# Delta-rule q, k and v turned by 32x32 blocks on DVE and over DRAM, decay chain with operands in PSUM, and a new slab order

## The chip, the core and the metric

The kernel runs on one core of one Trainium2 chip. Its engines are TensorE (PE; its weight loads are shown as PEld), VectorE (DVE), ScalarE (ACT), GpSimd (POOL) and SyncE (SP), which issues nearly all DMAs here. Each engine works through its own instructions in a fixed order and waits on semaphores for the others. SBUF is the on-chip working memory of 128 partitions; PSUM holds the results of matmuls. The metric is the device time of one execution in microseconds, as the median of several runs.

## What is computed

One layer of a hybrid encoder on 512 tokens of width 1024, in float32. The branch that the change touches is the gated delta rule: 8 heads of width 128, run forward and backward in chunks of 64 tokens.

```python
h = rms_norm(x, norm_pre)
(aq, ak, av, az, dq, dk, dv, db, da, dz, gate_att, gate_dn) = split_cols(h @ w_in)
...
qkv = silu(short_conv(concatenate([dq, dk, dv], -1), conv_w))      # 5 taps along the tokens
cq, ck, cv = qkv[..., :DN_KW], qkv[..., DN_KW:2 * DN_KW], qkv[..., 2 * DN_KW:]
qd = l2_norm(heads(cq)) * (DN_DK ** -0.5)
kd = l2_norm(heads(ck))
vd = heads(cv)
g = -exp(a_log) * softplus(da + dt_bias)                           # decay, per token, direction and head
beta = sigmoid(db)
o_dn = bidir_gated_deltanet(qd, kd, vd, g, beta)
o_dn = rms_norm(o_dn, dn_norm)
y_dn = (o_dn * silu(dz)) @ w_br_dn
...
mix = (sigmoid(gate_att) * y_att + sigmoid(gate_dn) * y_dn) @ w_out
x = x + rms_norm(mix, norm_post)
x = x + rms_norm(sigmoid(x @ w_ple_gate) * (p @ w_ple_proj), ple_norm)
```

Attention (8 query heads, 2 key heads, rotary) is the other branch; the change leaves it alone.

## The kernel before

**Products.** A float32 product of large matrices is made of three TensorE products of rounded parts: a weight slab of 1024 x 128 is loaded raw (wraw), ACT rounds it (whi), DVE or POOL subtract (wlo), and gemm_t (lines 529 to 531) sums lo x hi, hi x lo and hi x hi over 8 steps of 128 rows: 24 matmuls of 512 columns for one slab. gemm_n (548 to 550) and gemm_k (566 to 568) do the same for weights that stream. Small products (the delta rule's) are plain float32 matmuls, which appear as two TensorE instructions each; a transpose is one.

**The delta rule's way.** For each of 24 slabs dq0..7, dk0..7, dv0..7, conv_job runs gemm_t and spawns conv_tail. There, conv_silu2 scales the middle tap on ACT, adds four taps on DVE (scalar_tensor_tensor from PSUM), takes tanh on ACT and one more product on DVE. The result has features on partitions and tokens along a row. conv_tail then needs tokens on partitions: transposed (line 758) makes four 128x128 transposes on TensorE into a PSUM bank. For dk and dq, ACT squares them, DVE sums over the features (ssk, ssq), and for dk ACT copies the tile out (kn). For dv, DVE multiplies by the key norm into nv. k_stats and q_stats turn the sums into norms on POOL. Two groups of four heads follow each other: prep makes the decay factors E, phase_a the products kk and qk (938, 943), the masks, and the inverse of a triangular matrix by a chain of small DVE steps and by block products (1015 to 1063), and phase_b the walk over four chunks in two directions (kS 1097, oq 1108, pw 1117, pS 1135, oa 1149). In phase_b, kn is the stationary operand of line 1135; nv streams at line 1117 in the first step and is read by DVE at 1101 in the others.

**decay** (its small products at 665, 697 and 724) makes g and beta for all heads early on: 17 DVE operations of at most 64 elements a partition, on tiles gv and beta in SBUF, with an exponential and a logarithm on ACT between them. TensorE's line 697 waits for its end.

**What sets the order.** Nothing is scheduled at run time. While the program is built, the class Flow plays all these generators against each other with a planned duration for each operation, and each engine's instructions come out in the order of planned times. ORDER lists the slabs as TensorE's gemm stream takes them; PR holds priorities; caps holds the number of buffers (5 PSUM banks mm, 3 banks aux, 5 SBUF tiles f2). Two weight buffers and some spare ones (SPARE) let loads run ahead. W marks DVE operations that are planned so that POOL is idle beside them. warm_up (1773) makes TensorE transpose an identity until WARM, before the first product arrives.

## Time and profile before

| what | value |
|---|---|
| median of 3 runs | 764.97 us (763.32 to 765.44) |
| the profiled execution | 764.65 us, of which its span (first to last instruction) 762.9 us |
| granted TensorE clock, mean | 0.998 |
| bytes moved by DMA | 102.59 MB, 54472 packets |
| share of the 16 DMA engines, SP's queue | 41.0% |

The profile's page gives the busy time of each engine and its share of the span, the same in 40 slices, the chain of work that ended last (followed back from the last instruction, at each step to what released it), the groups of instructions by line with busy time, mean duration, the idle time ahead of them and what ended it, and the DMA issues with the time to landing. Views of the trace give waits (who waited for whom, in total, how often, the longest), timelines, and busy time in chosen windows. In a row, L758 is line 758 of the kernel; `mm<-ident,u` is an output tile and what it was made of. Operations recorded by the planner's helpers all carry a helper's line (L122, L97, L102), so they are told apart by tile.

### The profile page before, as it was taken

Reading aid. Unit: us, or ns where it says so; the run is one execution under the profiler, and the core shown is the slowest. Engines: PE = TensorE matmul, PEld = TensorE weight load, DVE = VectorE, ACT = ScalarE, POOL = GpSimd, SP = SyncE. Lnnn points to the kernel's source line nnn. Section 1 sums busy time; section 2 is a strip of 40 time slices with the busy share of each in tenths; the row PEclk is TensorE's granted clock in tenths of the full one; section 3 lists DMA queues with packets and bytes.
Section 4 is the critical chain, followed back from the end, with each engine's and each line's share of the span. In section 5 each row is a group of like instructions: output and inputs, shape, how many; then the busy total and the mean of one; then the engine's idle time right before and its main releaser. Section 6 shows DMA issues by size and latency. Waiting matters only on the chain.

```text
span 762.9 us, 11833 instructions
## 1 busy us (share of the span) xinstructions
PE 747.1 (98%) x4501; PEld 625.0 (82%) x4501; DVE 470.3 (62%) x907; ACT 346.4 (45%) x649; POOL 307.4 (40%) x277
## 2 busy tenths in 40 slices
PE   8999999999999999999999999999999999999996
PEld 7678888878789888888788888888888888888885
DVE  4788688886965567895874535437666743413334
ACT  6668635443644255423442245335566632332422
POOL 4735753103223255202711245557355434661511
PEclk9999999999999999999999999999999999999999
DMA  8851527636121136545311134435324255653313
GB/s 344 284 170 43 172 81 245 183 127 223 40 71 42 44 123 180 193 143 148 112 57 40 44 111 139 139 110 194 110 82 167 85 184 193 198 152 128 97 60 120
DMA packets 54472, 102.59 MB, mean 134 GB/s; under 512 B 21072, under 2 KB 22032, under 8 KB 54416
## 3 DMA queue, kind: packets, MB, share of 16 engines
q1 hardware_dynamic: 54128, 101.58, 41.0%
q8 instruction: 35, 0.57, 0.3%
q10 hardware_dynamic: 288, 0.26, 0.1%
q14 instruction: 21, 0.17, 0.1%
HBM read 82.92 MB, written 18.91 MB: 133 GB/s over the span
## 4 chain that ended last, share of the span: by engine, by line
PE 87%; DVE 4%; DMA 3%; ACT 3%; issue 1%; POOL 1%; SPq 0%; POOLq 0%; DVEq 0%; ACTq 0%
PE mm L529 16%; PE mm L531 15%; PE mm L530 15%; PE mm L550 4%; PE mm L548 4%; PE mm L549 4%; PE mm L567 2%; PE mm L568 2%; PE mm L566 2%; PE aux L1117 2%; PE mm L1472 2%; PE aux L1149 2%; PE aux L1097 1%; PE aux L1108 1%; PE aux L1135 1%
## 5 line engine op out<-in xcount | busy, mean ns | idle before, releaser
L102 POOL TENSOR_TENSOR wlo<-wraw,whi 128x1024 fp32r<-128x1024 f32 x52 | 124.5, 2395 | 256.9 <-ACT whi L122 221.8
L529 PE MATMUL mm<-u,wlo 128*128 128x512 f32 x504 | 204.7, 406 | 1.8 <-DVE f L122 1.1
L531 PE MATMUL mm<-u,whi 128*128 128x512 f32 x504 | 197.2, 391 | 0.0
L530 PE MATMUL mm<-u,whi 128*128 128x512 f32 x504 | 196.5, 390 | 0.0
L529 PEld LDWEIGHTS mm<-u,wlo 128*128 128x128 f32 x504 | 94.8, 188 | 20.6 <-issue 1.9
L531 PEld LDWEIGHTS mm<-u,whi 128*128 128x128 f32 x504 | 94.6, 188 | 20.8
L530 PEld LDWEIGHTS mm<-u,whi 128*128 128x128 f32 x504 | 95.0, 188 | 17.0
L122 ACT CAST whi<-wraw 128x1024 fp32r<-128x1024 f32 x64 | 67.1, 1049 | 85.8 <-PE mm L531 55.3
L122 DVE SCALAR_TENSOR_TENSOR f<-mm,cw,f 128x510 f32<-128x510 f32 (+1 forms) x96 | 71.8, 748 | 16.9 <-ACT f L122 14.2
L102 POOL TENSOR_TENSOR u<-wraw,u 128x1024 fp32r<-128x1024 f32 x23 | 55.0, 2398 | 22.2 <-ACT u L122 22.1
L122 DVE TENSOR_TENSOR u<-aux,u 128x512 f32<-128x512 f32 (+2 forms) x60 | 39.3, 670 | 24.8 <-ACT u L122 15.2
L548 PE MATMUL mm<-u,u 128*128 128x512 f32 (+1 forms) x136 | 52.0, 382 | 0.0
L550 PE MATMUL mm<-u,u 128*128 128x512 f32 (+1 forms) x136 | 51.4, 378 | 0.0
L549 PE MATMUL mm<-u,u 128*128 128x512 f32 (+1 forms) x136 | 51.3, 377 | 0.0
L122 ACT COPY c<-aux 128x512 f32<-128x512 f32 x18 | 10.6, 589 | 55.0 <-DVE f L122 35.0
L122 ACT CAST u<-aux 128x512 fp32r<-128x512 f32 (+1 forms) x28 | 15.6, 556 | 39.8 <-PE aux L1645 12.9
L566 PE MATMUL mm<-whi,u 128*128 128x512 f32 x80 | 31.6, 395 | 0.0
L567 PE MATMUL mm<-wlo,u 128*128 128x512 f32 x80 | 31.3, 391 | 0.0
L568 PE MATMUL mm<-whi,u 128*128 128x512 f32 x80 | 31.2, 390 | 0.0
L122 ACT ACTIVATE mm<-f 128x512 f32<-128x512 f32 x24 | 14.4, 599 | 35.5 <-DVE f L122 34.1
L122 ACT CAST u<-wraw 128x1024 fp32r<-128x1024 f32 x24 | 25.1, 1050 | 11.6 <-DMA wraw<-in_wn_dram 10.1
L550 PEld LDWEIGHTS mm<-u,u 128*128 128x128 f32 x136 | 25.6, 188 | 4.8
(258 smaller groups left out, 1456.1 us busy)
## 6 DMA issues: line engine op xcount, KB each, us to landing
wraw<-in_wt_dram SPq DMA_DIRECT2D x60, 512.0 KB, 3.6
wraw<-in_wn_dram SPq DMA_DIRECT2D x28, 512.0 KB, 3.9
u<-in_wt_dram SPq DMA_DIRECT2D x12, 512.0 KB, 5.5
u<-CI SPq DMA_DIRECT2D x16, 256.0 KB, 6.2
u<-in_x_dram SPq DMA_DIRECT2D x4, 512.0 KB, 7.0
u<-in_xT_dram SPq DMA_DIRECT2D x4, 512.0 KB, 8.2
eD<-u SPq DMA_DIRECT2D x8, 256.0 KB, 8.1
gate_dz<-go SPq DMA_DIRECT2D x8, 256.0 KB, 2.1
```

The costliest lines, as they stand in the source:

```text
L102: ins = fn(*a, **k)
L122: fn(*a, **k)
L529: pe.matmul(o, lo[:, k, :], mh(k), start=(k == 0), stop=False)
L530: pe.matmul(o, hi[:, k, :], ml(k), start=False, stop=False)
L531: pe.matmul(o, hi[:, k, :], mh(k), start=False, stop=(k == 7))
L548: pe.matmul(o, b, hi, start=(i == 0), stop=False)
L549: pe.matmul(o, a, lo, start=False, stop=False)
L550: pe.matmul(o, a, hi, start=False, stop=(i == 7))
L566: pe.matmul(o[t], b, hi, start=(k == 0), stop=False)
L567: pe.matmul(o[t], a, lo, start=False, stop=False)
L568: pe.matmul(o[t], a, hi, start=False, stop=(k == 7))
L1117: pe.matmul(pw[:, h, :], Vm[g][d][:, 4 * c + h, :], r[:, h, :], start=True, stop=True)
```

## The change

**Turning the tiles.** transposed goes out of conv_tail. In its place one DVE instruction transposes the 128 x 512 result in 32x32 blocks (small_blocks), into a tile T in which the four chunks j of a token row lie side by side. For dq, T is squared and summed over the 32 features of each block: four partial sums for each token on the four blocks of partitions. The function sums adds them by four small matmuls with `four`, four stacked 32x32 identities. For dk the same is done, and T is also written to DRAM in one DMA and read back in four (turned), which puts the blocks together: kn[g][:, h] now has the shape token x feature x chunk, so the feature step is four elements. For dv, T goes over DRAM into nv[g][:, h] in the same shape, and the product with the key norm is made there, by POOL or by ACT, whichever the planner finds free. phase_b reads the new shapes.

**decay.** The tiles z, e, u, dd and the unfinished beta move to a PSUM bank of mm; mk, a reciprocal, a product and max(z, 0) stay in SBUF (gs). The absolute value and the sign change of exp(a_log) go from DVE to ACT.

**Order.** A new ORDER, new priorities and a longer WARM (5.5 instead of 4.6: 20 transposes instead of 16); a few events wait for the later of two times.

```diff
 ORDER = """
-dq3 dk2 dq2 dk0 dk3 dq0 dk1 dq1 dz2 dk7 dq6 dz3 dv2 dv1 dv3 dz0
+dk3 dk1 vec dq2 dq0 dq1 dq3 dk2 dz4 dk0 dv3 dv1 dq4 dv2 dq5 az6
...
-PR = dict(dec=6, dm1=5, y=2, conv=9, gate=1, kv=2, q=4, head=9, ple=6, prep=6, tab=2)
+PR = dict(dec=3, dm1=3, y=2, conv=4, gate=5, kv=7, q=8, head=6, ple=6, prep=7, tab=9)
...
-WARM = 4.6
+WARM = 5.5
...
-    two = const([64, 32], "two")
-    pool.tensor_add(two, ident[0:64, 0:32], ident[0:64, 32:64])
+    four = const([128, 32], "four")
+    pool.tensor_add(four, ident[:, 0:32], ident[:, 32:64])
+    for i in (2, 3):
+        pool.tensor_add(four, four, ident[:, 32 * i:32 * i + 32])
+    two = four[0:64, :]
...
-    gv = const([128, 5, 2, 4, 8], "gv")
+    gs = const([128, 4, 2, 4, 8], "gs")
...
-        z, e, u, dd, mk = (gv[:, i] for i in range(5))
+        yield "get", "mm"
+        gv = bank("mm", [128, 5, 2, 4, 8])
+        z, e, u, dd, bt = (gv[:, i] for i in range(5))
+        mk, dr, es, zr = (gs[:, i] for i in range(4))
...
-        t = V(0.15, t, dve.scalar_tensor_tensor, out=e, in0=z, scalar=-1.0, in1=z, op0=ALU.mult, op1=ALU.max)
+        t = A(0.25, t, act.activation, e, z, AF.Abs)
...
+    def small_blocks(src, dep):
+        T = tile("f2", [128, 4, 32, 4])
+        return T, V(0.64, dep, dve.transpose, T.rearrange("p a q j -> p j a q"), src)
+
+    def turned(T, dep, name, dst):
+        B = dram(name, [4, 32, 4, 128])
+        tw = Q(2, dep, B.rearrange("P i a n -> (P i) a n"), T.rearrange("p a q j -> p a (q j)"))
+        t = tw
+        for a in range(4):
+            t = Q(WIDE, tw, dst[32 * a:32 * a + 32].rearrange("p (P q) j -> p P (q j)", P=4), B[:, :, a, :].rearrange("P i n -> i P n"))
+        return tw, t
...
-        yield "at", t + 0.3
-        pt = yield from transposed(dst)
+        yield "at", t - 0.5
+        yield "get", "f2"
+        T, t = small_blocks(dst, t)
         if kind == "dv":
-            free("f2")
+            free("f2", t)
+            tw, t = turned(T, t, f"B{kind}{hd}", nv[g][:, h])
+            free("f2", tw)
             yield "ev", nke
-            t = V(0.62, 0.0, dve.tensor_mul, nv[g][:, :, h, :], pt,
-                  nk[:, g, :, h].unsqueeze(2).to_broadcast([128, 4, 128]))
...
+            def scaled():
+                for j in range(4):
+                    act.activation(n_[:, :, j], n_[:, :, j], AF.Copy, scale=nk[:, g, j, h:h + 1])
+
+            return either(t, ("POOL", 1.1, pool.tensor_mul, n_, n_, by), ("ACT", 1.25, scaled))
         if kind == "dk":
-            ta = A(0.5, ta, act.copy, kn[g][:, :, h, :], pt)
+            tw, t2 = turned(T, t, f"B{kind}{hd}", kn[g][:, h])
...
+        ta = A(0.5, t, act.activation, sq, T, AF.Square)
+        t = V(0.62, ta, dve.reduce_sum, parts_[kind][:, g, :, h, :], sq.rearrange("p a q j -> p a j q"), axis=AX.X)
...
+    def sums(kind, g):
+        yield "at", F.now + 0.3
+        yield "get", "mm"
+        o = bank("mm", [128, 16])
+        for a in range(4):
+            pe.matmul(o[32 * a:32 * a + 32, :], four, parts_[kind][:, g, a].rearrange("p h j -> p (h j)"), start=True, stop=True)
+        yield "pe", 0.44
+        return o.rearrange("p (h j) -> p j h", h=4)
...
-                kn[g] = unit((6, 9)[g], [128, 4, 4, 128])
+                kn[g] = unit((6, 9)[g], [128, 4, 128, 4])
...
-                nv[g] = unit(u, [128, 4, 4, 128])
+                nv[g] = unit(u, [128, 4, 128, 4])
...
-                    in1=nv[g][:, c, h, :], op0=ALU.mult, op1=ALU.add))
+                    in1=nv[g][:, h, :, c], op0=ALU.mult, op1=ALU.add))
...
-                r = nv[g][:, c]
+                r = nv[g][:, :, :, c]
...
-                    pe.matmul(pS[:, h, :], kn[g][:, c, h, :], wd[:, h, :], start=True, stop=True)
+                    pe.matmul(pS[:, h, :], kn[g][:, h, :, c], wd[:, h, :], start=True, stop=True)
```

Three places in the engines' orders. First DVE in the decay chain, right behind TensorE's line 665 (f is the conv tile of the first slab, gv and h are the chain's tiles). Before:

```order
L122 TENSOR_TENSOR gv<-mm_378,h_88 128x64
L122 SCALAR_TENSOR_TENSOR gv<-gv 128x64
L122 SCALAR_TENSOR_TENSOR f_46_374<-mm_297,cw,f_46_374 128x510
L122 SCALAR_TENSOR_TENSOR f_46_374<-mm_297,cw,f_46_374 128x511 x2
L122 SCALAR_TENSOR_TENSOR f_46_374<-mm_297,cw,f_46_374 128x510
L122 TENSOR_SCALAR gv<-gv 128x64
L122 TENSOR_SCALAR beta<-beta 128x64
L122 TENSOR_SCALAR gv<-gv 128x64 x2
L122 SCALAR_TENSOR_TENSOR u_38_291<-mm_297,f_46_374 128x512
L122 TENSOR_TENSOR gv<-gv 128x64
L122 RECIPROCAL gv<-gv 128x64
L122 TENSOR_TENSOR gv<-gv 128x64 x3
```

Now, at the same place (mm_387 is the chain's PSUM bank):

```order
L122 TENSOR_TENSOR mm_387<-mm_382,h_90 128x64
L122 TENSOR_SCALAR gs<-mm_387 128x64
L122 SCALAR_TENSOR_TENSOR f_47_380<-mm_303,cw,f_47_380 128x510
L122 SCALAR_TENSOR_TENSOR f_47_380<-mm_303,cw,f_47_380 128x511 x2
L122 SCALAR_TENSOR_TENSOR f_47_380<-mm_303,cw,f_47_380 128x510
L122 TENSOR_SCALAR mm_387<-mm_387 128x64 x3
L122 TENSOR_SCALAR gs<-mm_387 128x64
L122 SCALAR_TENSOR_TENSOR u_38_296<-mm_303,f_47_380 128x512
L122 TENSOR_TENSOR mm_387<-mm_387,gs 128x64
L122 RECIPROCAL gs<-mm_387 128x64
L122 TENSOR_TENSOR gs<-mm_387,gs 128x64
L122 TENSOR_TENSOR mm_387<-mm_387,gs 128x64 x3
```

The sequence is nearly the same; each small operation now reads the PSUM bank. Second, DVE some 20 us later, among the conv tails of the first slabs (f are conv tiles and turned tiles, u_38, u_47 and u_56 the units of kT and qT, u_68 and u_69 those of E). Before:

```order
L122 TENSOR_REDUCE ssk<-f_73_550 128x4
L122 SCALAR_TENSOR_TENSOR u_38_291<-mm_430,f_64_498 128x512
L122 SCALAR_TENSOR_TENSOR f_74_566<-mm_499,cw,f_74_566 128x510
L122 SCALAR_TENSOR_TENSOR f_74_566<-mm_499,cw,f_74_566 128x511 x2
L122 SCALAR_TENSOR_TENSOR f_74_566<-mm_499,cw,f_74_566 128x510
L889 TENSOR_TENSOR u_69_512<-u_69_512,cj 128x512
L122 SCALAR_TENSOR_TENSOR u_47_375<-mm_499,f_74_566 128x512
L122 TENSOR_REDUCE ssq<-f_77_605 128x4
```

Now:

```order
L122 SCALAR_TENSOR_TENSOR u_56_437<-mm_438,f_63_498 128x512
L122 STREAM_TRANSPOSE f_72_542<-u_38_296 128x4x128
L122 SCALAR_TENSOR_TENSOR f_74_563<-mm_499,cw,f_74_563 128x510
L122 SCALAR_TENSOR_TENSOR f_74_563<-mm_499,cw,f_74_563 128x511 x2
L122 SCALAR_TENSOR_TENSOR f_74_563<-mm_499,cw,f_74_563 128x510
L122 STREAM_TRANSPOSE f_76_585<-u_56_437 128x4x128
L122 SCALAR_TENSOR_TENSOR u_56_437<-mm_499,f_74_563 128x512
L122 TENSOR_REDUCE sm<-f_76_585 128x4x4
L122 TENSOR_REDUCE partk<-f_77_591 128x4x4
L947 TENSOR_TENSOR u_69_512<-u_69_512,cj 128x512
```

Each conv tail has one 512-element operation more, the block transpose, and its reduction gives 4 x 4 sums instead of 4. Third, SP's queue at the start of the decay factors' loads (wraw and u_29 are weight slabs, u_68 and u_69 the tiles of E). Before:

```order
L122 DMA wraw_495<-in_wt_dram 128x1024
L122 DMA CI<-f_67_510 64x128
L122 DMA wraw_542<-in_wt_dram 128x1024
L122 DMA u_68_511<-CI 128x512
L122 DMA u_69_512<-CI 128x512
```

Now:

```order
L122 DMA wraw_507<-in_wt_dram 128x1024
L122 DMA Bdk_458<-f_58_457 128x512
L122 DMA CI<-f_67_510 64x128
L122 DMA wraw_547<-in_wt_dram 128x1024
L122 DMA u_39_297<-Bdk_458 32x4x128 x4
L122 DMA u_68_511<-CI 128x512
L122 DMA u_69_512<-CI 128x512
L122 DMA Bdk_543<-f_72_542 128x512
```

The write of a turned tile and the four reads back stand among the weight loads and the loads of E; the reads come one or two rows behind the write. Line numbers after the change: gemm_t is 533 to 535, sums 847, pw 1182, pS 1200.

More of the change, by code (lines that the diff above doesn't have):

```diff
@@ L173 @@
 EOUT = 24.0
+WIDE = 2.0
 LONG, NEAR = 0.6, 1.5
 X_DVE = ()
-WARM = 4.6
+WARM = 5.5
 W1 = 0
@@ L682, in decay @@
         t = V(0.15, t, dve.tensor_add, dd, dd, mk)
[L683 to L684 removed]
+        t = V(0.5, t, dve.reciprocal, dr, dd)
+        t = V(0.15, t, dve.tensor_mul, es, e, dr)
         t = V(0.15, max(t, tl), dve.tensor_add, u, u, mk)
[L686 to L692 removed]
+        t = V(0.15, t, dve.tensor_mul, u, u, es)
+        tz = V(0.15, th, dve.tensor_scalar, out=zr, in0=z, scalar1=0.0, scalar2=None, op0=ALU.max)
+        t = V(0.15, max(t, tz), dve.tensor_add, u, u, zr)
+        ta = A(0.2, ta, act.mul, h16[:, 0:16], h16[:, 0:16], -1.0)
+        tg = V(0.15, max(t, ta), dve.tensor_mul, gg, u, ha)
+        t = V(0.15, tb, dve.tensor_scalar, out=bt, in0=bt, scalar1=1.0, scalar2=None, op0=ALU.add)
+        t = V(0.5, t, dve.reciprocal, beta, bt)
+        free("mm", max(t, tg))
         yield "at", tg + 0.3
@@ L800, in k_stats @@
             yield "ev", e
+        o = yield from sums("dk", g)
+        t = V(0.2, 0.0, dve.tensor_scalar, out=nk[:, g], in0=o, scalar1=4.0 * EPS, scalar2=None, op0=ALU.add)
+        free("mm", t)
         yield "ev", dec
-        t = G(0.2, 0.0, pool.tensor_scalar, out=nk[:, g], in0=ssk[:, g], scalar1=4.0 * EPS, scalar2=None, op0=ALU.add)
         t = V(0.25, t, dve.reciprocal, kinv[:, g], nk[:, g])
@@ L816, in q_stats @@
             yield "ev", e
-        return rsqrt(16, 0.0, rq[:, g], 1.0, 4.0 * EPS, float(128 ** -0.5), ssq[:, g])
+        o = yield from sums("dq", g)
+        t = V(0.2, 0.0, dve.tensor_copy, rq[:, g], o)
+        free("mm", t)
+        return rsqrt(16, t, rq[:, g], 1.0, 4.0 * EPS, float(128 ** -0.5))
     conv_ev, stat_ev = {}, {}
@@ L900, in prep @@
         if away:
+            t = max(tE[g, d, c] for c in range(NT))
             free("u16", t)
@@ L947, in phase_a @@
                 t = V(0.62, tE[g, d, c], dve.tensor_mul, AT[g][d][:, 4 * c:4 * c + 4, :], qk, E)
-                t = V(0.62, t, dve.tensor_mul, E, kk, E)
-            free("aux", t)
-            free("aux", t)
+                tm = max(tm, V(0.62, t, dve.tensor_mul, E, kk, E))
+            ready = max(ready, tm)
+            free("aux", tm)
+            free("aux", tm)
+        t = ready
         dB, dW = dram(f"dB{g}", [128, 32, 32]), dram(f"dW{g}", [128, 32, 32])
```

63 lines of the change are left out of this document (34 added, 29 removed).

## The prediction

> **What bounds the kernel now.** I read the busy shares first, then the slices, then the chain that ended last.
>
> ```profile
> span 762.9 us, 11833 instructions
> PE 747.1 (98%) x4501; PEld 625.0 (82%) x4501; DVE 470.3 (62%) x907; ACT 346.4 (45%) x649; POOL 307.4 (40%) x277
> PE   8999999999999999999999999999999999999996
> PE 87%; DVE 4%; DMA 3%; ACT 3%; issue 1%; POOL 1%; SPq 0%; POOLq 0%; DVEq 0%; ACTq 0%
> ```
>
> TensorE is busy in every slice and is 87% of the chain. A busy engine that overlaps its own instructions could still hide a slack, so I looked at how it steps: in the chain in order of time a 512-column matmul holds 0.23 us, and by the view of waits little interrupts them:
>
> ```profile
> 201.37 0.23 PE mm L530
> ```
>
> ```profile
> PE aux L697 <- DVE gg L122: 1.4, 1, 1.4
> ...
> PE mm L758 <- DVE f L122: 1.1, 1, 1.1
> PE mm L529 <- DVE f L122: 1.1, 1, 1.1
> PE aux L1097 <- ACT c L122: 0.5, 1, 0.5
> ...
> PE aux L1028 <- issue: 0.2, 1, 0.2
> ```
>
> Beside the first 6.27 us and the tail behind the last matmul (code that does not change), the list of ten holds 1.4 + 1.1 + 1.1 + 0.5 + 0.4 + 0.4 + 0.3 + 0.2 = 5.4 us of waiting. So the kernel is a TensorE queue, and a TensorE instruction taken out of it shortens the run by its own slot, as long as nobody becomes late.
>
> **The change part by part.** Base: the profiled execution, 764.65 us (span 762.9 plus 1.75 around it); the median shown is 764.97, 0.3 above it.
>
> *Transposes off TensorE.* `transposed` goes: 24 conv tails with four transposes each.
>
> ```profile
> 50.77 0.44 PE mm L758 x4
> L758 PE MATMUL mm<-ident,u 128*128 128x128 f32 x64 | 9.7, 273 | 0.1
> ```
>
> Two thirds of them, 64, are in the second row; its busy sum (9.7) counts the 0.27 us latency of each group, while the chain shows the slot, 0.44 for four. 24 x 0.44 = **-10.6**. The 1.1 us wait goes with its instruction.
>
> *Sums over four partition blocks.* Four groups of four small matmuls (32 TensorE instructions, as a float32 matmul is two) are new. The nearest rows bound them:
>
> ```profile
> 44.01 1.08 PE aux L697 x8
> 202.53 0.65 PE aux L1028 x48
> 214.80 2.01 PE aux L1048 x64
> ```
>
> With 128 stationary columns, (1.08 - 0.28) / 7 = 0.114 us each, or 3.6 in all; 32x32 tiles step by (0.65 - 0.19) / 47 = 0.01, 0.3 in all. 64x64 tiles at (2.01 - 0.22) / 63 = 0.028 lie nearest to 32 stationary columns: **+0.9**, bounds 0.3 and 3.6.
>
> *Start.* The first stream of matmuls is slow:
>
> ```profile
> 1.41 3.68 PE L1773 MATMUL mm<-ident 128*128 128x128 f32 x16 [1.41 <-POOL ident masks.py:199]
> 6.27 0.76 PE L1238 MATMUL mm<-u,u 128*128 128x512 f32 x1 [1.18 <-DVE u L97]
> ...
> 9.39 0.44 PE L1239 MATMUL mm<-u,u 128*128 128x512 f32 x1
> ```
>
> ```profile
> 19.39 1.24 DVE wlo L97
> ```
>
> From 6.27 to 9.39 seven steps take 3.12 us instead of 7 x 0.23 = 1.6. Twenty warm-up transposes instead of 16 end at 1.41 + 20 x 0.23 = 6.0, so the gap of 1.18 nearly closes and the first real matmul still starts at 6.27. At best 1.5 us is won; but the chain at 17 to 22 us lies on DVE, ACT and POOL (the 19.39 row), so most of an early finish would be waited away there. I take **-0.5**, bounds 0 and -1.5. [...]
>
> *Decay chain in PSUM.* DVE's small operations stand still behind POOL here:
>
> ```profile
> 31.70 2.35 DVE L122 SCALAR_TENSOR_TENSOR gv<-gv 128x64 f32<-128x64 f32 x1
> 33.99 3.11 DVE L122 SCALAR_TENSOR_TENSOR f<-mm,cw,f 128x510 f32<-128x510 f32 x4
> 37.02 1.72 DVE L122 TENSOR_SCALAR gv<-gv 128x64 f32<-128x64 f32 x1
> ...
> 40.55 2.71 DVE L122 TENSOR_TENSOR gv<-gv 128x64 f32<-128x64 f32 x3
> ```
>
> ```profile
> 31.56 2.41 POOL L102 TENSOR_TENSOR wlo<-wraw,whi 128x1024 fp32r<-128x1024 f32 x1 [1.04 <-ACT whi L122]
> 33.93 4.75 POOL L102 TENSOR_TENSOR u<-u,u 128x1024 fp32r<-128x1024 f32 x2
> 40.38 2.40 POOL L102 TENSOR_TENSOR wlo<-wraw,whi 128x1024 fp32r<-128x1024 f32 x1 [1.70 <-ACT whi L122]
> ```
>
> Operations of 64 elements take 2.35 and 1.72 us and end when POOL's two-input subtractions end (34.05 at 33.97, 38.74 at 38.68), and the three at 40.55 are held up likewise until 42.78; the conv steps at 33.99, with one operand in PSUM, run through POOL's 4.75 us at their usual 0.75 each. With z, e, u, dd and beta in PSUM every small operation of this chain has an operand there. That frees about 2.1 + 1.5 + 2.1 = 5.7 us of DVE (each stall less the 0.2 of a free one). The way from L665 to L697, 12.5 us now, becomes some 7, and TensorE still has 45 matmuls there (10.3 us, 0.44 less than now), so the 1.4 us wait goes: with L758's, **-2.5**.
>
> *DVE and the queue.* DVE gains 24 block transposes and loses eight products.
>
> ```profile
> L122 DVE SCALAR_TENSOR_TENSOR f<-mm,cw,f 128x511 f32<-128x511 f32 x48 | 36.0, 750 | 1.7
> L122 DVE STREAM_TRANSPOSE c<-u 32x512 f32<-32x512 f32 x8 | 5.6, 703 | 0.1
> L122 DVE TENSOR_REDUCE ssk<-f 128x4 f32<-128x512 f32 x8 | 5.4, 683 | 0.8 <-ACT f L122 0.7
> L122 DVE TENSOR_TENSOR u<-mm,nk 128x512 f32<-128x512 f32 x8 | 5.5, 682 | 0.3 <-PE mm L758 0.3
> 30.30:122.00 91.70, 90.20 (x463) 75.47 (x463) 73.89 (x112) 54.92 (x116) 54.65 (x46) 1.00 0.43 135
> ```
>
> 24 x 0.70 - 8 x 0.68 = +11.4 us of DVE, hidden beside TensorE if DVE keeps up. The tightest stretch runs from the decay chain to the last E product of group 0. There the new order has 13 conv tails (13 x (4 x 0.75 + 0.69) = 48), 13 block transposes (9.1), 10 reductions (6.8), 21 other 512-element operations (14.4) and about 3 us of small ones: **81 us of DVE against about 91 us of TensorE** (354 matmuls at 0.23, eight times 0.89 for the kk and qk groups, 3 us else). Today about the same stretch is the window quoted last: 73.89 of 91.70 us busy. DVE keeps up, with 10 us to spare. Uncovered, each microsecond beyond those 10 is one of the total. The 80 new DMAs go through SP's queue; what they bring is needed only by phase_b, which in the new order has more than 60 us of TensorE work ahead of it behind the last dv slab of either group, so their landing costs nothing. What remains of today's waits (5.4 - 2.5 = 2.9) I keep, and since every place in the order is new I add **+3.0** for new waits, bounds -2.9 (all gone) and +8.
>
> Sum: -10.6 + 0.9 - 0.5 - 2.5 + 3.0 = -9.7, so 764.65 - 9.7 = **755.0 us**. With every term at its good end: -10.6 + 0.3 - 1.5 - 2.5 - 2.9 = -17; but all of these together is unlikely, and I end the forecast's own range at 750, and at 759 above.
>
> **The rivals.** The new tiles kn and nv keep the four chunks of a token row side by side, so that TensorE reads kn[:, h, :, c] and nv[:, h, :, c], and DVE the squares and nv, one element in every 16 bytes. No TensorE row of before reads so. DVE has one pair: the solve's first step has 30 elements in 30 rows, 128 bytes apart, its last 30 side by side; and 58 elements in pairs:
>
> ```profile
> L973 DVE TENSOR_TENSOR blk<-blk,blk 128x30 f32<-128x30 f32 x1 | 0.2, 216 | 0.0
> L973 DVE TENSOR_TENSOR blk<-blk,blk 128x30 f32<-128x30 f32 x1 | 0.2, 191 | 0.0
> L973 DVE TENSOR_TENSOR blk<-blk,blk 128x58 f32<-128x58 f32 x1 | 0.2, 221 | 0.0
> L973 DVE TENSOR_TENSOR blk<-blk,blk 128x58 f32<-128x58 f32 x1 | 0.2, 220 | 0.0
> ```
>
> Apart costs (216 - 191) / 30 = 0.83 ns per element more; pairs (221 to 220) cost nothing. Thirty elements are few, and a row's end could be what costs.
>
> *Rival 1, slower: strided reads on TensorE.* L1135 loads kn as its weights.
>
> ```profile
> L1135 PE MATMUL aux<-f,u 128*128 128x128 f32 x96 | 13.0, 279 | 0.2
> 226.96 0.89 PE aux L1135 x8
> ```
>
> If each of its 96 loads of 128 columns, and the 32 first-chunk passes that stream nv, took 128 x 0.83 = 0.107 us more, that is 128 x 0.107 = 13.6 us: 755.0 + 13.6 = **768.6**. It decides from about 0.7 of that price (9.7 / 128 = 0.076 us a load), where it eats the whole gain. Against it: those slots (0.89 / 8 = 0.11) may have room to hide a slower read. Chance 0.20. [...]
>
> *Rival 2: DVE becomes the bound.* The same price on DVE alone: 23 transposes and reductions in the tight stretch x 512 x 0.83 ns = 9.8 us, all of its spare 10, and 48 steps of phase_b that read nv at +0.1 = 5. Half of this waited for, 7 us: **762**. The five PSUM banks are held longer, and TensorE waits at L529 and in kk and qk. Chance 0.20.
>
> *Rival 3: SP's queue.* Each of 16 heads writes to DRAM and, a row or two later, reads back, and the read waits in the queue until the write has landed; weight loads stand behind it.
>
> ```profile
> gate_dz<-go SPq DMA_DIRECT2D x8, 256.0 KB, 2.1
> L122 ACT CAST whi<-wraw 128x1024 fp32r<-128x1024 f32 x64 | 67.1, 1049 | 85.8 <-PE mm L531 55.3 <-PE mm L568 11.8 <-issue 8.4
> ```
>
> A landing is 2.1 us and the weight split waits for TensorE's buffers, not for loads, so 2 us of delay fits. If a quarter of it came through: 16 x 0.5 = 8, **763**. Chance 0.10.
>
> **How the numbers follow.** Forecast 755.0 (750 to 759) 0.50; rival 1 (766 to 772) 0.20; rival 2 (757 to 765) 0.20; rival 3 (757 to 767) 0.10. A measurement tells 0.3% from no change: below 762.7 is faster, above 767.3 slower. Faster: 0.50 + 0.13 + 0.05 = 0.68. Within: 0.03 of rival 1, 0.07 of rival 2, 0.05 of rival 3 = 0.15. Slower: 0.17. The range 750 to 767.5 leaves out the upper part of rival 1 (0.16) and about 0.03 below.
>
> **What would show it.** TensorE's busy time near 737 and waits under 6 us: forecast. L1200's groups of eight at 0.89 us: rival 1 is wrong; near 1.7: right. Block transposes at 0.70 and reductions at 0.68: rival 2 is wrong; near 1.1, with waits of L533 for DVE: right. ACT casts waiting for wraw: rival 3. The small operations on mm at 0.2 us each confirm the decay step, and the starts between 6.27 and 9.4 the warm-up. I am wrong if TensorE's slot does not shrink with the transposes, or if new waits exceed 8 us.

## The result, and the profile after

| | before | after |
|---|---|---|
| median | 765.21 us (763.32 to 765.72, 4 runs) | 784.32 us (782.69 to 785.27, 4 runs) |
| ratio | | 1.0252, 95% interval 1.0227 to 1.0277 |
| span of the profiled execution | 762.9 us | 782.9 us |
| TensorE busy / span less busy | 747.1 / 15.8 us | 757.3 / 25.6 us |

The change makes the kernel 2.5% slower; forecast were 755.0 us, and 767.5 as the upper end. The page of the changed kernel, its busy shares and its chain:

```profile
span 782.9 us, 11886 instructions
PE 757.3 (97%) x4441; PEld 633.8 (81%) x4441; DVE 490.8 (63%) x923; ACT 350.7 (45%) x649; POOL 321.0 (41%) x284
PEclk9999999999999999998999999999999999999998
PE 81%; DVE 7%; DMA 4%; ACT 3%; issue 2%; POOL 2%; SPq 1%; POOLq 0%; DVEq 0%; ACTq 0%
```

TensorE has 60 instructions fewer (96 transposes less, 32 for the sums and 4 of the warm-up more) and is busy 10.2 us *longer*; beside that it stands idle 9.8 us longer. Both parts have to be explained. The first is read from the groups of instructions by line and shape (busy time in us, mean of one in ns, then the idle time ahead):

```profile
L1200 PE MATMUL aux<-f,u 128*128 128x128 f32 x96 | 24.1, 394 | 0.1
L1182 PE MATMUL aux<-u,u 128*128 128x128 f32 x32 | 7.7, 404 | 0.0
L122 DVE STREAM_TRANSPOSE f<-u 128x512 f32<-128x512 f32 x16 | 17.7, 1103 | 0.1
L122 DVE TENSOR_REDUCE partk<-f 128x16 f32<-128x512 f32 x8 | 8.5, 1063 | 1.3 <-ACT f L122 1.3
L1166 DVE SCALAR_TENSOR_TENSOR c<-aux,nec,u 128x128 f32<-128x128 f32 x48 | 17.8, 435 | 5.6 <-PE aux L1162 5.6
L821 ACT ACTIVATE u<-u,nk 128x128 f32<-128x128 f32 x24 | 10.5, 516 | 7.8 <-DMA u<-Bdv 7.8
```

L1200 is the line that was L1135 (kn as weights): 394 ns in place of 279. The nv stream of the first chunk (L1182) takes 404 ns; before it was L1117, with 275:

```profile
L1117 PE MATMUL aux<-u,u 128*128 128x128 f32 x32 | 3.9, 275 | 0.0
```

Block transposes take 1.10 us and reductions 1.06, not 0.70 and 0.68; phase_b's product with nv takes 435 ns in place of 342. All of these touch one element in every 16 bytes. In the chain, a group of eight of L1200 holds 1.74 us where it held 0.89:

```profile
285.59 1.74 PE aux L1200 x8
```

The second part, from the view of waits of TensorE:

```profile
PE mm L533 <- DVE u L97: 5.7, 1, 5.7
PE mm L533 <- POOL wlo L102: 3.5, 3, 1.8
PE mm L533 <- DVE wlo L97: 2.5, 2, 2.1
PE aux L1092 <- issue: 2.3, 2, 1.8
```

The wait of 5.7 us ends at 364.54. Followed back through the chain in order of time:

```profile
350.96 6.41 DMA wraw<-in_wn_dram
357.38 1.81 DMA u<-Bdv
359.25 0.17 ACT u L821
359.43 0.21 issue
359.64 2.17 ACT u L821 x5
361.81 0.48 ACT go L122
362.29 0.94 ACT u L122
363.25 1.24 DVE u L97
364.54 0.79 PE mm L533
365.33 0.43 PE mm L534
```

nv comes back from DRAM behind a weight load; ACT stands before its scaling (L821), with the gate of a dz slab and the weight split queued behind it, and TensorE waits for that split. When TensorE goes on, its matmuls start every 0.43 us in place of 0.23: the granted clock is down. In windows of 20 us it is below 1.00 in two places ahead of the tail (200 to 220: 0.91; 360 to 380: 0.83). TensorE loses less than 20 x 0.09 + 20 x 0.17 = 5.2 us by it, since the second of these stretches (granted 0.50 from 362.4 to 369.2) begins while TensorE still stands idle: by the starts, 8 steps from 212.10 to 215.62 take 3.5 us and 12 steps from 364.54 to 369.55 take 5.0, in place of 0.23 each, so 1.7 + 2.3 = 4.0 us. Before, the clock is below 1.00 in no window ahead of the tail:

```profile
PEclk9999999999999999999999999999999999999999
```

Now:

```profile
340.00:360.00 20.00, 18.89 (x85) 15.26 (x84) 17.96 (x39) 8.12 (x15) 3.96 (x2) 1.00 0.59 171
360.00:380.00 20.00, 15.46 (x59) 12.62 (x60) 13.25 (x33) 8.41 (x13) 3.30 (x2) 0.83 0.52 176
```

### The profile page after: what moved, and what is told of

Same layout as the page of the kernel before. It is cut to its first block, busy times and chain, and to the rows that moved or that the text cites. A ratio compares the mean times of both kernels' runs of the same rounds, so it can differ in the third digit from the quotient of the medians.

```text
span 782.9 us, 11886 instructions
## 1 busy us (share of the span) xinstructions
PE 757.3 (97%) x4441; PEld 633.8 (81%) x4441; DVE 490.8 (63%) x923; ACT 350.7 (45%) x649; POOL 321.0 (41%) x284
## 4 chain that ended last, share of the span: by engine, by line
PE 81%; DVE 7%; DMA 4%; ACT 3%; issue 2%; POOL 2%; SPq 1%; POOLq 0%; DVEq 0%; ACTq 0%
PE mm L533 14%; PE mm L534 13%; PE mm L535 13%; PE mm L554 4%; PE mm L552 4%; PE mm L553 4%; PE aux L1200 3%; DVE f L122 3%; PE mm L571 2%; PE mm L570 2%; PE aux L1182 2%; PE mm L572 2%; PE mm L1537 2%; PE aux L1214 2%; PE aux L1162 1%
## 5 line engine op out<-in xcount | busy, mean ns | idle before, releaser
L102 POOL TENSOR_TENSOR wlo<-wraw,whi 128x1024 fp32r<-128x1024 f32 x56 | 134.3, 2398 | 230.1 <-ACT whi L122 191.0
L533 PE MATMUL mm<-u,wlo 128*128 128x512 f32 x512 | 207.3, 405 | 6.2 <-POOL wlo L102 3.5
L535 PE MATMUL mm<-u,whi 128*128 128x512 f32 x512 | 200.4, 391 | 0.0
L534 PE MATMUL mm<-u,whi 128*128 128x512 f32 x512 | 200.4, 391 | 0.0
L533 PEld LDWEIGHTS mm<-u,wlo 128*128 128x128 f32 x512 | 96.7, 189 | 27.2 <-POOL wlo L102 5.1
L535 PEld LDWEIGHTS mm<-u,whi 128*128 128x128 f32 x512 | 96.5, 189 | 20.9
L534 PEld LDWEIGHTS mm<-u,whi 128*128 128x128 f32 x512 | 96.8, 189 | 17.8
L122 DVE SCALAR_TENSOR_TENSOR f<-mm,cw,f 128x510 f32<-128x510 f32 (+1 forms) x96 | 71.4, 745 | 13.1 <-ACT f L122 10.6
L102 POOL TENSOR_TENSOR u<-wraw,u 128x1024 fp32r<-128x1024 f32 x22 | 52.7, 2399 | 15.5 <-ACT u L122 15.5
L122 DVE TENSOR_TENSOR u<-aux,u 128x512 f32<-128x512 f32 (+2 forms) x60 | 39.4, 670 | 23.8 <-ACT u L122 17.5
L122 ACT COPY c<-aux 128x512 f32<-128x512 f32 x18 | 10.6, 587 | 57.4 <-DVE f L122 32.0
L102 POOL TENSOR_SCALAR_AFFINE_SELECT u<-u 128x512 f32<-128x512 f32 x16 | 10.1, 637 | 57.1 <-DMA u<-CI 22.3
L533 PE MATMUL mm<-u,u 128*128 128x512 f32 x64 | 26.4, 412 | 5.7 <-DVE u L97 5.7
L554 PEld LDWEIGHTS mm<-u,u 128*128 128x128 f32 x136 | 25.6, 188 | 4.8
L553 PEld LDWEIGHTS mm<-u,u 128*128 128x128 f32 x136 | 25.6, 188 | 4.6
```

Source lines behind the costliest of these rows:

```text
L102: ins = fn(*a, **k)
L122: fn(*a, **k)
L533: pe.matmul(o, lo[:, k, :], mh(k), start=(k == 0), stop=False)
L534: pe.matmul(o, hi[:, k, :], ml(k), start=False, stop=False)
L535: pe.matmul(o, hi[:, k, :], mh(k), start=False, stop=(k == 7))
L553: pe.matmul(o, a, lo, start=False, stop=False)
```

## The experiments

Two theories stand at the start. **S**: the step of 16 bytes is the price, directly on TensorE and by DVE's lateness in the waits. **Q**: the waits come from the round trip over DRAM and from what queues behind it. Each ratio below is against the kernel before, timed beside it on the same chip; the chip differs from one series to another, so series are compared by their ratios.

**One: take the steps away and keep the program.** The changed kernel's instructions, order and dependencies stay; only the addresses change, in three ways (each engine's sequence is the same in all four profiles). The quarters that are read then hold features and chunks mixed, so these three kernels (and x4_late below) do not compute the reference's delta rule.

```diff
# e1_pe_flat: TensorE
+    def flat(x, c):
+        return x.rearrange("p f j -> p (f j)")[:, c * 128:(c + 1) * 128]
-                pe.matmul(pw[:, h, :], Vm[g][d][:, 4 * c + h, :], r[:, h, :], ...)
+                pe.matmul(pw[:, h, :], Vm[g][d][:, 4 * c + h, :], flat(nv[g][:, h], c) if s == 0 else r[:, h, :], ...)
-                    pe.matmul(pS[:, h, :], kn[g][:, h, :, c], wd[:, h, :], ...)
+                    pe.matmul(pS[:, h, :], flat(kn[g][:, h], c), wd[:, h, :], ...)
# e2_dve_flat: DVE
-        ... dve.transpose, T.rearrange("p a q j -> p j a q"), src)
+        ... dve.transpose, T.rearrange("p a q j -> p (a q j)"), src)
-        ... dve.reduce_sum, ..., sq.rearrange("p a q j -> p a j q"), axis=AX.X)
+        ... dve.reduce_sum, ..., sq.rearrange("p a q j -> p (a q j)").rearrange("p (a j q) -> p a j q", a=4, j=4), axis=AX.X)
-                    in1=nv[g][:, h, :, c], op0=ALU.mult, op1=ALU.add))
+                    in1=flat(nv[g][:, h], c), op0=ALU.mult, op1=ALU.add))
# e3_all_flat: both, and the scaling of nv on ACT and POOL
-                    act.activation(n_[:, :, j], n_[:, :, j], AF.Copy, ...)
+                    act.activation(flat(n_, j), flat(n_, j), AF.Copy, ...)
```

> The changed kernel, but TensorE reads kn as weights (L1200 of the changed kernel) and nv in each recurrence's first chunk (L1182) as contiguous quarters of 128 elements instead of one element in every 16 bytes. The quarters hold features and chunks mixed, so the delta rule's output isn't the reference's; instructions, order and dependencies stay. Theory S (strided reads on TensorE cost about 14 us): groups of eight of L1200 fall from 1.74 to 0.89 us (12 groups, -10.2), groups of sixteen of L1182 from 3.6 to 1.8 (-3.7), and the time is 784.3 - 13.9 = 770 us (768 to 773). Rival (the slots are long for another reason, such as DMA traffic beside them or the lower granted clock): the groups stay above 1.5 and the time stays at 782 to 785.

> The changed kernel, but DVE's 24 block transposes write contiguously, the 16 reductions read contiguously, and phase_b's 48 products read nv contiguously; TensorE, ACT and POOL still read with the step of 16 bytes. The data are arranged otherwise, so the delta rule's output isn't the reference's. DVE's busy time falls by 24 x 0.40 + 16 x 0.39 + 48 x 0.09 = 20 us. Theory D (DVE is late because of these steps, and TensorE's 16 us of waits with the clock drops behind them follow from it): the waits of L533 for DVE and POOL go, and the time is 784.3 - 8 to 14 = 770 to 776. Rival Q (the waits come from the round trip over DRAM and the instructions queued behind it on SP and ACT): 781 to 785, with the wait near 363 us still there.

> Both of the first two edits, and ACT and POOL scale nv contiguously as well: no engine reads or writes kn, nv, T or the squares with a step of 16 bytes any more (the delta rule's output isn't the reference's). If the step of 16 bytes is all that failed: 784.3 - 13.9 (TensorE) - 8 to 14 (waits and clock) = 756 to 762, near the 755 of the prediction. If queues and the new order make the waits: 766 to 771, with 10 us or more of TensorE waits behind the first matmul.

| | median us | ratio, 95% | span | TensorE busy | span less busy |
|---|---|---|---|---|---|
| after | 784.32 | 1.0252 (1.0227 to 1.0277) | 782.9 | 757.3 | 25.6 |
| e1_pe_flat | 769.09 | 1.0058 (1.0038 to 1.0078) | 768.0 | 742.5 | 25.5 |
| e2_dve_flat | 779.62 | 1.0191 (1.0162 to 1.0220) | 779.2 | 756.9 | 22.3 |
| e3_all_flat | 763.79 | 0.9992 (0.9973 to 1.0011) | 762.4 | 740.3 | 22.1 |

With contiguous reads TensorE's two groups are back at the durations of before, and its busy time falls by 757.3 - 742.5 = 14.8 us, as does the time (0.0194 of 764 = 14.8):

```profile
L1203 PE MATMUL aux<-f,u 128*128 128x128 f32 x96 | 13.3, 281 | 0.5 <-DVE f L122 0.4
L1185 PE MATMUL aux<-u,u 128*128 128x128 f32 x32 | 4.1, 275 | 0.0
```

So S holds for TensorE. DVE's edit takes its transposes back to 704 ns and phase_b's product to 344, but only 4.7 us of time come with it (0.0061 of 764), under the 8 to 14 expected: most of TensorE's waits were not DVE's slowness. All steps together (e3, with those of ACT and POOL) are worth 0.0260 of 764 = 19.9 us, and then the changed program is **as fast as the kernel before, no faster**: between the two ranges expected. Nearly 9 us of the forecast gain are still missing. In e3 the largest wait stands at the same place, with no stepped access left in the chain:

```profile
335.61 3.92 DMA Bdv<-f
339.59 0.32 SPq L122
339.96 0.44 SPq L122
340.45 0.42 SPq L122
340.92 4.79 DMA u<-Bdv
345.82 0.52 ACT u L822 x2
346.44 0.48 ACT u L822 x2
347.02 1.26 ACT u L822 x4
348.28 0.48 ACT go L122
348.76 0.94 ACT u L122
349.73 1.24 DVE u L97
351.01 0.79 PE mm L533
```

From DVE's tile to the first scaled element 345.82 - 335.61 = 10.2 us pass; the planner reckons with about half of that. That is Q's picture: write, issue and read take 10 us, and ACT is held by it.

**Two: the same data in runs of 32.** Can a real kernel avoid the step? Here T is chunk by chunk, so that DVE writes runs of 32; kn has its chunks one behind the other, written and read back in eight DMAs with pieces of 128 bytes; nv has runs of 32.

```diff
-        T = tile("f2", [128, 4, 32, 4])
-        return T, V(0.64, dep, dve.transpose, T.rearrange("p a q j -> p j a q"), src)
+        T = tile("f2", [128, 4, 4, 32])
+        return T, V(0.64, dep, dve.transpose, T.rearrange("p a j q -> p j a q"), src)
...
-                kn[g] = unit((6, 9)[g], [128, 4, 128, 4])
+                kn[g] = unit((6, 9)[g], [128, 4, 4, 128])
-                nv[g] = unit(u, [128, 4, 128, 4])
+                nv[g] = unit(u, [128, 4, 4, 4, 32])
-                    pe.matmul(pS[:, h, :], kn[g][:, h, :, c], wd[:, h, :], start=True, stop=True)
+                    pe.matmul(pS[:, h, :], kn[g][:, h, c], wd[:, h, :], start=True, stop=True)
```

> The changed kernel with its data laid out so that each access has runs of 32 or 128 elements: the block transpose writes chunk by chunk in runs of 32, kn holds its four chunks one behind the other (its DRAM block is written by four DMAs of a quarter each and read back in pieces of 128 bytes), nv holds runs of 32 features of one chunk. The whole reference is computed. If runs of 32 cost what contiguous ones cost: the time of the kernel with every access contiguous, within 3 us (756 to 762 if steps are all that failed). If the smaller pieces of the DMAs delay the read back: kn lands later, but it is needed only in phase_b, so nothing more. Rival: a piece of 32 elements still costs DVE or TensorE half of the step's price: 770.

Measured: 773.21 us, ratio 1.0114 (1.0088 to 1.0139). The accesses are as cheap as contiguous ones: transposes 0.70 us, reductions 0.68, the nv product 344 ns. Still it is 9.4 us behind e3, and above every time expected. With the edit the planner placed everything anew, and TensorE waited elsewhere: for a weight split on POOL (4.5 us, clock 0.83 from 60 to 80 us) and in the walk over the chunks (clock 0.92 and 0.74 in the two windows from 420 to 460 us). This was the first hint that the place of instructions is worth as much as the change.

**Three: one part at a time.** The new table of numbers without the new path; the decay chain without the rest; e3 with the scaling of nv queued later; the runs of 32 with the old table.

```diff
# x1_order: the kernel before with ORDER, OUT0, PR and WARM of the changed kernel
# x3_decay: the kernel before with the decay chain of the changed kernel (gv a bank of mm)
# x4_late: e3_all_flat, with
-            yield "at", t - 0.5
+            yield "at", t + 5.0
             n_ = nv[g][:, h]
# x6_runs_oldorder: e4_runs with ORDER, OUT0 and PR of the kernel before
```

> The kernel before with the change's table only: the new slab order, output order, priorities and 20 warm-up transposes in place of 16; transposes, decay chain and all data as before. Theory O (the new order itself brings the waits that remain when every access is contiguous): slower than the kernel before by 4 to 8 us, 769 to 773, with TensorE waits of 10 us or more behind the first matmul. Rival P (the waits belong to the new path over DVE and DRAM, and the order is harmless): 762 to 766, of which the start gives up to -1.

> The kernel before with the decay chain's operands in PSUM only (and its absolute value and negation on ACT); everything else as before. The prediction's step: DVE's small operations no longer wait for POOL, each takes about 0.2 us, and TensorE's 1.4 us wait of L697 goes: 764.0 - 1.4 = 762.6 (761.5 to 763.5). Rival: the bank of five that the chain now holds makes TensorE wait elsewhere, or the planner fills the place otherwise: 764 or more.

> The kernel with every access contiguous, and the scaling of nv put into its engine's queue 5.5 us later by the planner's clock (the planner expects the DRAM round trip at some 5 us, the trace shows 10). Theory H (ACT stands before the scaling with the gate of the dz slab queued behind it, and TensorE with its next slab behind that): ACT's waits for u<-Bdv go from 8.8 to under 3 us, TensorE's wait of 4.1 us near 347 goes with the slow matmuls behind it, and the time is 763.8 - 4 to 7 = 757 to 760. Rival: TensorE waits as long for the loads behind SP's queue, 762 to 765.

> The kernel with runs of 32 or 128 elements (the whole reference is computed) with the slab order, output order and priorities of the kernel before. If the new order makes the waits (theory O): 773.2 falls to 755 to 760, and the slow matmuls of phase_b between 400 and 470 us go. If the path over DVE and DRAM makes them (P): 766 to 774.

| | median us | ratio, 95% | TensorE busy | span less busy |
|---|---|---|---|---|
| x1_order | 772.47 | 1.0120 (1.0086 to 1.0154) | 749.3 | 19.5 |
| x3_decay | 761.69 | 0.9972 (0.9961 to 0.9983) | 745.1 | 15.2 |
| x4_late | 768.60 | 1.0064 (1.0042 to 1.0087) | 744.0 | 22.1 |
| x6_runs_oldorder | 791.54 | 1.0364 (1.0326 to 1.0402) | 752.8 | 38.6 |

The decay chain does what was forecast. In the timelines of DVE and POOL in x3_decay, small operations with an operand in PSUM run through POOL's subtractions at about 0.25 us each, and L697's wait is gone:

```profile
33.11 4.77 POOL L102 TENSOR_TENSOR u<-u,u 128x1024 fp32r<-128x1024 f32 x2
...
36.21 0.76 DVE L122 TENSOR_SCALAR mm<-mm 128x64 f32<-128x64 f32 x3
...
39.61 0.77 DVE L122 TENSOR_TENSOR mm<-mm,gs 128x64 f32<-128x64 f32 x3
```

The new order with the old path is slower by about 9 us (theory O), though TensorE's idle time grew by 19.5 - 15.8 = 3.7 us and not by the 10 expected. The old order with the new path is slower still, by 28, far outside the ranges of both theories: order and path belong together, and on these plans neither half explains the loss by itself. x4_late is a miss that teaches: ACT's waits for the round trip are gone (8.8 us in e3; the view of ACT's waits has no row with Bdv any more), the wait of 4.1 us before L533 is gone too, and the kernel is 4.8 us *slower* than e3. The idle time is the same 22.1 us, now in phase_b:

```profile
PE aux L1186 <- DVE f L122: 1.4, 1, 1.4
PE aux L1204 <- DVE f L122: 1.4, 2, 0.8
PE aux L1218 <- DVE blk L1210: 1.2, 1, 1.2
```

```profile
440.00:460.00 20.00, 18.16 (x108) 16.31 (x108) 12.35 (x35) 4.03 (x7) 0.85 (x3) 0.90 0.00 1
420.00:440.00 20.00, 15.48 (x98) 13.12 (x98) 7.75 (x23) 3.89 (x6) 2.52 (x2) 0.93 0.27 93
```

From 429 to 449 us TensorE's timeline has no matmul of a slab between the steps of the walk; e3 has 39 in the same stretch. The job queued later changed the plan, and in the new plan the filler no longer stands in the place that needs it.

**Four: a part of the path, with the old order.** q alone (which never goes to DRAM), q and k, and the longer warm-up.

```diff
# y1_dq: x3_decay, and in conv_tail
+        if kind == "dq":
+            yield "at", t - 0.5
+            yield "get", "f2"
+            T = tile("f2", [128, 4, 4, 32])
+            t = V(0.64, t, dve.transpose, T.rearrange("p a j q -> p j a q"), dst)
+            ta = A(0.5, t, act.activation, T, T, AF.Square)
+            t = V(0.62, ta, dve.reduce_sum, parts_[kind][:, g, :, h, :], T, axis=AX.X)
...
# y2_dqk: the same for dk, with kn over DRAM as in e4_runs
# y4_warm: x3_decay, and
-WARM = 4.6
+WARM = 5.5
```

> The kernel before with the decay chain in PSUM and with q alone taken off TensorE's transposes: DVE's block transpose in runs of 32, squares and reduction on it, sums of the four partition blocks by the four small matmuls; k and v as before, the order as before. Nothing of q passes over DRAM. The whole reference is computed. By the prediction's terms: 8 x 0.44 = 3.5 us less on TensorE, +0.3 for the sums, so 761.7 - 3.2 = 758.5 (757 to 760) if no new wait comes (theory P: the waits belong to the path over DRAM and to ACT's scaling). Rival O (any such edit shifts the planner's program away from the order fitted to it): 760 to 766.

> As the kernel with q alone, and k as well: kn goes by four DMAs of a quarter to DRAM and by four back, v stays on TensorE. Another 8 x 0.44 = 3.5 us less on TensorE, and eight copies (ACT) less: 755 to 756 if DRAM's round trip is covered, as the prediction said for all of them. If the round trip makes the waits (SP's queue in front of weight loads): 760 to 770, with ACT casts waiting for wraw.

> The kernel before with the decay chain in PSUM and 20 warm-up transposes in place of 16, alone. The prediction's step: 761.7 - 0.5 (0 to -1.5), the wait of L1242 before the first real matmul under 0.4 us and the slow starts after it fewer than six. Rival: what is won at the start is waited away at 17 us: 761.5 to 762.

y1_dq took 767.37 us, ratio 1.0045 (1.0032 to 1.0059), in place of 758.5: 5.7 us slower than x3_decay, with 16 TensorE instructions fewer and no DRAM in the way. So the way over DRAM cannot be the only source of the waits (theory P). Its longest new wait is one of 2.6 us that ends near 69 us, for a weight split on POOL, whose ACT half came 1.3 us later than in x3_decay (65.34 against 64.08) since a 2 us job for the decay factors E now stands right ahead of it, at 62.90; matmuls at 0.43 follow. y2_dqk took 786.42 us, ratio 1.0296 (1.0262 to 1.0331); what it computes differs from the reference, for a reason that I did not find, so nothing rests on it. y4_warm took 761.46 us, ratio 0.9971 (0.9959 to 0.9983), the same as x3_decay's 0.9972, as its rival expected. The first real matmul starts at 5.60 us and at 5.54 in x3_decay, against 6.27 in the kernel before.

**Five: a control for the planner.** If every edit brings new waits, an edit that changes nothing but the plan should as well. Theory **F**: the table (order and priorities) is fitted to one plan.

```diff
# nb_b: the kernel before; ne_b: e4_runs; na_b: the changed kernel
-            t = V(0.75, t, dve.scalar_tensor_tensor, out=y[:, a:b], ...
+            t = V(0.76, t, dve.scalar_tensor_tensor, out=y[:, a:b], ...
# nb_c: the kernel before; ne_c: e4_runs
-        t2 = A(0.52, t + 0.1, act.activation, po, y, AF.Tanh, scale=0.5)
+        t2 = A(0.54, t + 0.1, act.activation, po, y, AF.Tanh, scale=0.5)
# m1_measured: e4_runs, with 0.70 for the block transpose (0.64) and 0.68 for the reduction (0.62)
# m2_measured_b: both of m1_measured and ne_b
```

> The kernel before, with nothing changed but the planner's own estimate of a conv step on DVE (0.76 in place of 0.75 us), which moves the planned places of instructions on all engines. Theory F (the slab order is fitted to one plan, and any other plan waits more): slower than the kernel before by 3 to 10 us (767 to 774), with TensorE waits at new places. Rival (plans are alike and the path over DVE and DRAM makes the waits): 762 to 766.

> The same with another estimate: the tanh of the conv tail on ACT (0.54 in place of 0.52 us). Theory F: 767 to 774 and waits at other places than in the last run; rival: 762 to 766.

> The kernel with runs of 32 or 128 elements (whole reference computed), with the estimate of a conv step at 0.76 us. Theory F: the time moves by several us from 773, to either side (760 to 785), with PE's instructions taking the same time as before the edit and only the waits and the clock behind them changed. Rival: within 2 us of 773.

> The kernel with runs of 32 or 128 elements, with the estimate of the tanh at 0.54 us. Theory F as in the last run: 760 to 785, not within 2 us of 773.

> The changed kernel itself, with nothing changed but the planner's estimate of a conv step (0.76 in place of 0.75 us). If steps and plan are separate prices: TensorE's rows stay at 1.74 us for eight loads and the waits change; the time is 784 plus or minus 10. If this plan is a good one, as it was for the kernel with runs of 32: 758.8 + 20 = 779.

> The kernel with runs of 32 or 128 elements (whole reference computed), the planner's estimates of the block transpose and the reduction set to the measured 0.70 and 0.68 us (0.64 and 0.62 before). If truer estimates make a better plan: 755 to 760. If a plan is a matter of chance: anywhere from 757 to 775.

> As the last run, and the conv step's estimate at 0.76 us as well. If truer estimates make a better plan: 755 to 759; if it is a matter of chance: 757 to 775.

| | median us | ratio, 95% | TensorE busy | span less busy |
|---|---|---|---|---|
| nb_b | 766.49 | 1.0041 (1.0030 to 1.0053) | 748.3 | 17.1 |
| nb_c | 766.22 | 1.0021 (1.0002 to 1.0041) | 748.6 | 16.2 |
| na_b | 777.42 | 1.0178 (1.0162 to 1.0194) | 755.8 | 20.2 |
| e4_runs | 773.21 | 1.0114 (1.0088 to 1.0139) | 746.9 | 25.5 |
| ne_b | **758.80** | **0.9934** (0.9913 to 0.9956) | 738.3 | 18.6 |
| ne_c | 774.10 | 1.0135 (1.0114 to 1.0156) | 744.4 | 28.2 |
| m1_measured | 768.57 | 1.0062 (1.0045 to 1.0079) | 743.7 | 23.6 |
| m2_measured_b | 775.80 | 1.0145 (1.0113 to 1.0177) | 749.1 | 27.2 |

The kernel before loses 0.2 to 0.4% (1.6 to 3.1 us) by one or two hundredths of a microsecond in an estimate: less than the 3 to 10 us expected, but in both runs to the worse. The kernel with runs of 32 moves by 0.0211 of 764 = 16 us over five plans, from 758.8 to 775.8, with the same 4441 instructions on TensorE in each. Truer estimates gave one better plan (768.6 against e4_runs' 773.2) and one worse (775.8 against ne_b's 758.8). On the good plan, ne_b, TensorE is busy for 738.3 us, ACT no longer waits for the round trip, and the granted clock is full up to the tail:

```profile
span 756.9 us, 11929 instructions
PE 738.3 (98%) x4441; PEld 616.4 (81%) x4441; DVE 476.5 (63%) x926; ACT 344.3 (45%) x638; POOL 316.9 (42%) x283
PEclk9999999999999999999999999999999999999998
PE 91%; DVE 3%; DMA 2%; ACT 1%; POOL 1%; issue 1%; SPq 0%; POOLq 0%; DVEq 0%; ACTq 0%
```

ne_b leaves nothing out and beats both kernels: 0.9934 of the kernel before. It is the best of five plans; the other four are slower than the kernel before, so what it shows is that about half of the forecast gain can be reached (5.0 of 9.7 us), not that the new path wins as such. And the changed kernel on another plan (na_b) is 0.0074 of 764 = 5.7 us faster than on its own, with the step still in every row: TensorE's busy time there is 755.8, 17.5 us above ne_b's.

## Why the prediction was wrong

The forecast of 755.0 us has a span of 755.0 - 1.75 = 753.2 us, of which TensorE's busy time is 747.1 - 10.6 + 0.9 - 0.5 = 736.9 and the rest 16.3. Against that the changed kernel has 782.9 = 753.2 + 14.8 (stepped reads on TensorE, from e1) + 5.6 (e1's 742.5 less 736.9; by the starts, matmuls at the lowered clock make some 3.4 of it) + 9.3 (idle, 25.6 less 16.3). Of the 29.3 us between forecast and measurement, 19.9 go with the step of 16 bytes (e3).

- **Transposes, -10.6, and sums, +0.9: right in the main.** ne_b and y4_warm both have the decay chain in PSUM, twenty warm-up transposes and no lowered clock ahead of the tail; TensorE's busy time differs by 746.4 - 738.3 = 8.1 us, where 9.7 was forecast. The 32 matmuls of the sums have weights of 32 columns and 16 columns to stream, and the last eight hold 0.19 us of the chain.
- **Start, -0.5: not confirmed.** In the changed kernel the slow starts after the first real matmul end at 7.5 us instead of 9.4, and DVE's first product of h starts at 15.97 instead of 17.00. But nb_b, the kernel before on another plan with its sixteen transposes, has no slow stretch either, and that product starts at 16.04:

```profile
5.62 0.47 PE L1238 MATMUL mm<-u,u 128*128 128x512 f32 x1 [0.75 <-DVE u L97]
...
7.66 0.39 PE L1243 MATMUL mm<-u,u 128*128 128x512 f32 x1
```

Eight steps take 2.04 us, where seven took 3.12. x3_decay is alike (16.14). So the slow stretch follows sixteen transposes at times only, and the prediction took one profiled execution of it for the usual case; alone on x3_decay the longer warm-up made no measurable difference.
- **Decay chain, -2.5: the mechanism right, the size not contradicted.** Of it 1.4 belong to the wait that x3_decay removes, and x3_decay gains 0.0028 of 763 = 2.1 us. That is no more than the 1.6 to 3.1 us by which an estimate alone moved the kernel before.
- **Rival 1 is the step that failed first, by its chance and not by its price.** The sum put strided reads on TensorE at nothing. TensorE's stepped loads were priced at 128 x 0.107 = 13.6 us and measured at 14.8; eight loads of 128 columns take (1.74 - 0.89) / 8 = 0.106 us more each. I gave this 0.20, for the reason that the slots might have room. But the only rows of before that had a step at all charged 0.83 ns an element, and nothing in the profile showed room. By the row that I quoted, the strided price belonged into the sum and the free read among the rivals. No run had shown the price on TensorE. The trace of the changed kernel shows it: 0.106 us / 128 = 0.83 ns an element on TensorE's loads.
- **Rivals 1 and 2 were taken as alternatives, though they have one cause.** It is one kind of access at about one price per element, and the runs found it on both engines (0.83 ns on TensorE's loads, 0.78 on DVE's transposes); the case that went with it was 755.0 + 13.6 + 7 = 775.6, not 768.6 or 762, and the range had to reach there. In e3 the two together, with ACT's and POOL's steps, cost 19.9.
- **Rival 2, DVE becomes the bound: its prices right, its effect two thirds.** Transposes and reductions cost 0.40 and 0.38 us more each, as its 0.43 said, and phase_b's 48 products 0.09. DVE's busy time rose, but contiguous accesses on DVE alone gave back 4.7 us, of the 7 forecast.
- **Rival 3, the queue: its mechanism is there**, on ACT more than on SP: the round trip takes 10 us, where I had counted one landing of 2.1, since write, issue and read follow each other (3.9, 1.4 and 4.8 us in e3's chain) and a read can land behind a weight load (one of 6.4 us in the changed kernel's chain). In e3 it ends in the largest wait. That it *costs* those microseconds is not shown: with the scaling queued later that wait went, and the time did not fall.
- **New waits, +3.0 with an upper bound of 8: mis-sized.** In e3, where no step is left, TensorE is (22.1 - 16.3) + (740.3 - 736.9) = 9.2 us above the forecast, which holds the +3.0 already: some 12 us in its place, beyond the bound. Of the second bracket, 2.4 us are matmuls at the lowered clock (12 steps in 5.1 us behind the wait of 4.1); the other 1.0 is about what ne_b, with no lowered clock ahead of the tail, is above the forecast as well (738.3 - 736.9 = 1.4). I had sized the term from the waits of a table fitted to the old program, and priced a wait at its own length alone. Over five plans of the same work the spread is 16 us. What stays open is which property makes a plan good; the runs show that neither truer estimates nor removing the longest wait does it by itself.

## What to carry to other kernels

An access pattern that the profile of before shows only once, in a small row, is still the best evidence there is: put its price into the sum for every engine that will read so, and together, since one cause has one truth. Lay tiles out so that the engines' innermost run is long (here one element in 16 bytes cost a block transpose 1103 ns, runs of 32 cost 701 to 704), and let the DMA take the short pieces, as in ne_b, where kn is read back in pieces of 128 bytes and TensorE's longest wait is 1.8 us. In a kernel whose static order has been fitted, any edit can be a new draw of the order: before a loss or gain of 1% is put down to the edit, time two or three plans of each version that differ in nothing but an estimate.

## What the runs showed of the hardware

- One element in 16 bytes cost each of the four engines 0.7 to 1.0 ns per element: TensorE's weight loads 0.83 ns ((1.74 - 0.89) us / 8 / 128), its moving operand 1.0 ns ((404 - 275) / 128), DVE's transposes writing so 0.78 ns ((1103 - 704) / 512, against e2), its reductions 0.74 ((1063 - 683) / 512, against those of before), its product with nv 0.73 ((435 - 342) / 128), ACT's copy that reads and writes so 1.0 ns ((516 - 388) / 128, against L973's on contiguous tiles of that shape), GpSimd's product, whose second operand steps so (the key norms), 1.0 ((1550 - 1037) / 512, against its product of that shape for E). I had thought it likely that TensorE, which overlaps its loads with matmuls (625.0 and 747.1 us in a span of 762.9 before), hides it.
- Runs of 32 elements cost none of it: DVE's transposes 704 ns (e4) and 701 (ne_b), its reductions 0.68 us, its product with nv 344 and 343 ns; twelve instructions of the nv stream hold 1.50 us in ne_b, and fourteen contiguous ones 1.73 before, 0.12 each in both.
- Behind each of the six waits of 4 us or more of which a view shows the stretch the granted clock was down: 5.7 us in the changed kernel (0.83 from 360 to 380 us), 5.9 in e1 (0.85 from 340 to 360), 4.1 in e3 (0.83 from 340 to 360), 4.5 in e4 (0.83 from 60 to 80), 5.6 in m1_measured (0.83 from 60 to 80), and 5.7 in e2, by the starts (eleven steps of 0.40 to 0.43 us from 362.53 on, then 0.23). So these waits cost TensorE more than themselves: after the 4.1 us of e3 the next ten matmuls start 0.43 us apart in place of 0.23, which is 2.4 us on top.
- Shorter waits were followed by it at times: in the changed kernel one of 1.8 us by 3.4 us at 0.50 (212.2 to 215.6), one of 2.1 us was not (140 to 160 us: 1.00). In the walk over the chunks the clock fell with no wait above 1.4 us, where no slab's matmuls stood between the steps (x4_late, 420 to 460 us: 0.93 and 0.90).
